# Moving operands read in turn from two halves, two front fillers fewer, and two row blocks begun early, in a hybrid encoder layer

## The chip, the cores and the metric

The kernel runs on one core of one Trainium2 chip. The metric is the device time of one execution in microseconds, and lower is better. Three timed runs of the kernel before gave 859.51, 858.84 and 859.25 us, a median of 859.25.

## The reference

One layer of a bidirectional encoder, on two sequences of 256 tokens (together T = 512 columns) with D = 1024 channels, all in float32. Cut to what matters:

```python
h = rmsnorm(x) ; proj = h @ w_in            # 9952 columns: q|k|v, decays, gates, latents, queries
# branch A: depthwise conv + SiLU on q, k, v; gated delta rule forwards and backwards, 8 heads
o_gdn = rmsnorm(o_fwd + o_bwd) * silu(z_gdn)
# branch B: latent attention, 8 heads, low-rank q and kv, rotary part
o_mla = softmax(q_full @ k_full.T * scale) @ v * silu(z_mla)
# branch C: attention of 4 heads into 256 memory tokens
o_mem = softmax(qx @ km.T * scale) @ vm * silu(z_mem)
merged = (sigmoid(g0) * (o_gdn @ w_br_gdn) + sigmoid(g1) * (o_mla @ w_br_mla)
          + sigmoid(g2) * (o_mem @ w_br_mem))
y = rmsnorm(x + merged @ w_out)
```

## The kernel before

Activations lie feature-major: a tile has 128 channels on the partitions and the 512 tokens of both sequences on the columns. A product `h @ w` is made in row blocks of 128 output channels. Weights and activations are kept as two parts, a rounded high part and the rest (names with `hh`/`hl`, `wh`/`wl`), in the format fp32r, and a product is three passes: high by high, high by low, low by high. So a row block over 1024 input channels is 24 matmuls of 512 columns, `gemm` at line 246. Each has its own stationary 128x128 piece of the weight, and the moving operand is the activation tile.

Each block's weight is loaded by SP (`wr_`, two buffers), rounded by ACT to `wh_` (line 210), and the rest is split off by DVE to `wl_` (line 214). The high part is needed by the block's first 16 matmuls, the low part by the last 8.

There are three stages. The **front** (`front`) makes the memory keys and values, the latents and both attentions. Its PE order is chosen by the scheduling layer from priorities. `fills(n)` takes n row blocks from a list of fillers (`plan`): q/k/v blocks of the delta rule with their convolution (`qkv_tile`), gates (`gate_tile`, names `g`), and so on. These stand between attention steps, so that TensorE has work while ACT and DVE do a softmax. While fillers are made, `prepare` issues a few steps of the first solver preparation (`gdn_prep`): a chain of DVE operations on `tt` and `tm`, 31 rounds long, for four heads each.

The **middle** (`middle`) runs the delta rule. Its PE order is written out by a planner, `weave`: it keeps a planned time, lets each chain (preparation, loads, decays, two solver lanes, output, norm) issue its next step when its planned time has come, and fills the time between with filler matmuls. `gemm` yields the planned cost of each matmul, and a chain step yields its own cost and the delay until its next. `can` says when a filler may start. The names are `kk` for key products, `u`, `xs`, `us`, `x` for solver steps, `o` for a head's output, `so` for its sum of squares, `rob` for the norm row that comes back by way of DRAM (`d_n`), `xg` for the normed head.

The **back** (`back`) multiplies the eight heads `xg` by the first branch's weight (`bg`, eight row blocks), adds up the merge, and runs the output product `y` with the final norm (`output`). `bm` are the second branch's row blocks, `be` the third's. Blocks `bm` and `bg` take their last input channels last, so that late heads hold up only the end of a block.

PSUM has eight banks. In the front, three are for `gm` (gemm outputs), two for `kk`, three for `ms`; from the middle on four are for `gm` and two for each of two `ms` tags.

Of the kernel before, what the change touches and what calls it, by code (L numbers as in the profile page):

```python
# [7 lines left out]
F32 = mybir.dt.float32  # L8
# [5 lines left out]
P = 128  # L14
# [71 lines left out]
def prep(i):  # L86
# [12 lines left out]
    def col(a):  # L99
# [27 lines left out]
        "xT": fm(x), "xn": tm(x), "memT": fm(mem),  # L127
# [29 lines left out]
class Layer:  # L157
# [41 lines left out]
    def weight(self, src, n, name, pool=None):  # L199
# [7 lines left out]
        kw = {} if pool else {"tag": "wh", "bufs": 2}  # L207
        hi = (pool or self.p0).tile([P, 1024], F32R, name="wh_" + name, **kw)
        with self.tc.high_priority(offset=60):
            self.wround = nc.scalar.activation(hi[:, :n], raw[:, :n], AF.Copy).ins  # L210
            kw = {} if pool else {"tag": "wl", "bufs": 2}
            lo = (pool or self.p0).tile([P, 1024], F32R, name="wl_" + name, **kw)
            eng = nc.vector
            d = eng.tensor_tensor(lo[:, :n], raw[:, :n], hi[:, :n].bitcast(F32), op=ALU.subtract)  # L214
            if eng is nc.vector:
                self.wsplit = d.ins
# [17 lines left out]
    def gemm(self, src, nk, xs, name, m=P, ps=None):  # L234
# [10 lines left out]
        for (a, j), k in order:  # L245
            nc.tensor.matmul(ps[:m], a[:, k * m:(k + 1) * m], xs[k][j],  # L246
                             start=n == 0, stop=n == 3 * nk - 1)
            n += 1
            yield 0.234
# [106 lines left out]
    def mem_v(self):  # L356
# [28 lines left out]
        for k, (raw, wr) in enumerate(raws):  # L385
# [10 lines left out]
            for i, (a, b) in enumerate(((0, hi), (1, hi), (0, lo))):  # L396
                for tb in range(4):
                    t = slice(tb * P, (tb + 1) * P)
                    nc.tensor.matmul(vps[tb], ms[k][a][:, t], b[:, :512],  # L399
# [24 lines left out]
    def mem_kt(self, h):  # L424
# [3 lines left out]
            nc.scalar.activation(kt, ps, AF.Copy)  # L428
# [60 lines left out]
    def rotate(self, dst, src, table):  # L489

        n = table.shape[0]
        self.nc.vector.tensor_tensor(dst.rearrange("p (s t) -> p s t", s=2), src.rearrange("p (s t) -> p s t", s=2),
                                     table.unsqueeze(1).to_broadcast([n, 2, 256]), op=ALU.mult)

    def rope_key(self):
# [13 lines left out]
        self.rotate(t[0:64], ps[0:64], cs[0:64])  # L509
        self.rotate(u[0:32], ps[32:64], sn[32:64])  # L510
        self.rotate(u[32:64], ps[0:32], sn[0:32])
# [138 lines left out]
    def mla_rope(self, g):  # L650
# [6 lines left out]
        for j, (p1, p2, op) in enumerate(((pa, pb, ALU.subtract), (pb, pa, ALU.add))):  # L657
            t, u = self.tb("rt"), self.tb("ru")
            self.rotate(t, p1, self.cos)
            self.rotate(u, p2, self.sin)  # L660
# [14 lines left out]
    def mla_v(self, g):  # L675
# [4 lines left out]
        for tb in range(4):  # L680
# [5 lines left out]
            for a, j in ((hi, 0), (hi, 1), (lo, 0)):  # L686
                for k in range(2):
                    nc.tensor.matmul(ps, self.kl[k][j][:, t], a[:, k * 512:(k + 1) * 512],
# [7 lines left out]
    def mla_qk(self, hh, between):  # L696
        A = self.A
        r = []
        for w, nk, xs, n in ((A["w2"], 2, self.kl, "kn"), (A["w3"], 3, self.ql, "qn")):
# [9 lines left out]
            self.split(ps, hi, lo)  # L709
# [39 lines left out]
    def qkv_tile(self, h, part):  # L749
# [4 lines left out]
        if part < 2:  # L754
# [3 lines left out]
            if part == 0:  # L758
                self.k_done.add(h)
            return  # L760
# [854 lines left out]
```

## Time and profile before

| | us |
|---|---|
| median of the timed runs | 859.25 |
| the profiled execution's own time | 859.05 |
| its span in the profile | 857.3 |
| TensorE busy | 845.6 |
| VectorE (DVE) busy | 573.4 |
| ScalarE (ACT) busy | 451.9 |
| GpSimd (POOL) busy | 145.4 |

The span is the time from the first to the last instruction of the core, and the execution's own time has 1.75 us more around it. PE is TensorE's matmuls; PEld are the loads of stationary operands, which run beside them; DVE, ACT, POOL and SP are the vector, scalar, GpSimd and sync engines. Matmuls are pipelined, so a record of 0.4 us can begin 0.23 us after the one before it: what counts is the distance from start to start. In the chain of waits, each row has its start, its length and what ran, followed back from the last instruction. A row of the stage table has the stretch, and for each engine the busy time and the number of instructions in it. In a row of a timeline, the bracket at the end tells how long the engine sat idle before the instruction and what ended that.

### The profile page before, as it was taken

How to read it: one execution, taken by the hardware profiler on the slowest of the kernel's cores; microseconds unless marked ns; L12 is line 12 of the kernel's file. 1: busy time of each engine (PE TensorE's matmuls, PEld its weight loads, DVE VectorE, ACT ScalarE, POOL GpSimd, SP SyncE). 2: the span in 40 equal slices, each digit the busy share in tenths (PEclk: the TensorE clock that was granted, in tenths of full speed). 3: DMA queues.
4: the chain of work that ended last, by engine and by line, in shares of the span. 5: the costliest groups of instructions: out<-in, count | busy, mean ns of one | idle time of the engine just before them, and what ended most of it. 6: DMA issues, size and time to landing. Idle time of an engine off the chain costs nothing.

```text
span 857.3 us, 13230 instructions
## 1 busy us (share of the span) xinstructions
PE 845.6 (99%) x4822; PEld 698.4 (81%) x4822; DVE 573.4 (67%) x1021; ACT 451.9 (53%) x891; POOL 145.4 (17%) x135
## 2 busy tenths in 40 slices
PE   9999999999999999999999999999999999999997
PEld 7878888888888888878788888888888888888886
DVE  7776347687599998457689998684555544346543
ACT  7655455455474465546775748666663632223232
POOL 0200111000100002072101254213110002332121
PEclk9999999999999999999999999999999999999999
DMA  9422222442425525363334365546445447375332
GB/s 326 141 79 87 86 81 68 139 138 75 103 77 164 137 90 146 116 191 129 109 103 122 117 189 174 152 134 180 132 122 160 138 134 250 118 241 160 116 98 99
DMA packets 68273, 116.10 MB, mean 135 GB/s; under 512 B 24048, under 2 KB 31600, under 8 KB 68208
## 3 DMA queue, kind: packets, MB, share of 16 engines
q1 hardware_dynamic: 46560, 104.51, 38.6%
q10 hardware_dynamic: 21648, 10.75, 4.6%
q8 instruction: 38, 0.62, 0.3%
q14 instruction: 27, 0.22, 0.1%
HBM read 95.09 MB, written 16.99 MB: 131 GB/s over the span
## 4 chain that ended last, share of the span: by engine, by line
PE 95%; DVE 2%; ACT 1%; issue 1%; DMA 1%; POOL 0%; POOLq 0%; ACTq 0%; DVEq 0%; SPq 0%
PE gm_qkv L246 16%; PE gm_g L246 16%; PE gm_z L246 8%; PE gm_bm L246 5%; PE gm_bg L246 5%; PE gm_za L246 5%; PE y L1256 5%; PE vm L399 3%; PE gm_be L246 3%; PE gm_qm L246 3%; PE gm_km L246 3%; PE kk L971 3%; PE o L1121 2%; PE gm_qn L246 2%; PE gm_cq L246 2%; PE s_a L308 2%
## 5 line engine op out<-in xcount | busy, mean ns | idle before, releaser
L745 DVE SCALAR_TENSOR_TENSOR kq<-cz,prm,kq 128x510 f32<-128x510 f32 (+1 forms) x64 | 48.1, 752 | 6.0 <-ACT kq L738 5.0
L246 PE MATMUL gm_qkv<-hh,wh_qkv 128*128 128x512 f32 x192 | 51.1, 400 | 0.5 <-ACT wh_qkv L210 0.5
L246 PE MATMUL gm_g<-hl,wh_g 128*128 128x512 f32 x192 | 51.5, 399 | 0.0
L246 PE MATMUL gm_g<-hh,wl_g 128*128 128x512 f32 x192 | 51.3, 398 | 0.0
L246 PE MATMUL gm_g<-hh,wh_g 128*128 128x512 f32 x192 | 51.1, 401 | 0.1
L246 PE MATMUL gm_qkv<-hh,wl_qkv 128*128 128x512 f32 x192 | 50.3, 397 | 0.0
L246 PE MATMUL gm_qkv<-hl,wh_qkv 128*128 128x512 f32 x192 | 49.7, 396 | 0.0
L214 DVE TENSOR_TENSOR wl_qkv<-wr_qkv,wh_qkv 128x1024 fp32r<-128x1024 f32 x24 | 31.1, 1297 | 25.9 <-ACT wh_qkv L210 10.1
L214 DVE TENSOR_TENSOR wl_g<-wr_g,wh_g 128x1024 fp32r<-128x1024 f32 x24 | 30.1, 1254 | 22.0 <-PE gm_g L246 11.7
L246 PEld LDWEIGHTS gm_qkv<-hl,wh_qkv 128*128 128x128 f32 x192 | 35.8, 188 | 8.2
L246 PEld LDWEIGHTS gm_qkv<-hh,wh_qkv 128*128 128x128 f32 x192 | 35.3, 188 | 8.9 <-ACT wh_qkv L210 1.2
L246 PEld LDWEIGHTS gm_qkv<-hh,wl_qkv 128*128 128x128 f32 x192 | 35.5, 188 | 7.8
L246 PEld LDWEIGHTS gm_g<-hl,wh_g 128*128 128x128 f32 x192 | 35.4, 188 | 7.7
L246 PEld LDWEIGHTS gm_g<-hh,wl_g 128*128 128x128 f32 x192 | 35.3, 188 | 7.5
L246 PEld LDWEIGHTS gm_g<-hh,wh_g 128*128 128x128 f32 x192 | 35.1, 188 | 7.8 <-ACT wh_g L210 0.3
L210 ACT ACTIVATE wh_qkv<-wr_qkv 128x1024 fp32r<-128x1024 f32 x24 | 25.4, 1058 | 29.1 <-PE gm_qkv L246 8.6
L1256 PE MATMUL y<-wh_wo,mh 128*128 128x512 f32 (+1 forms) x144 | 39.9, 370 | 0.0
L210 ACT ACTIVATE wh_g<-wr_g 128x1024 fp32r<-128x1024 f32 x24 | 25.4, 1060 | 26.0 <-PE gm_g L246 11.6
L961 POOL TENSOR_TENSOR kl<-kq,kh 128x512 fp32r<-128x512 f32 x16 | 22.8, 1427 | 94.8 <-ACT kh L959 94.8
L1226 POOL TENSOR_TENSOR mg<-mg,lg 128x512 f32<-128x512 f32 x16 | 27.2, 1700 | 59.0 <-DVE lg L1225 59.0
L246 PE MATMUL gm_bm<-xa,wh_bm 128*128 128x512 f32 x128 | 33.5, 398 | 0.0
L246 PE MATMUL gm_bg<-xg,wh_bg 128*128 128x512 f32 x128 | 32.5, 395 | 0.0
(432 smaller groups left out, 2199.5 us busy)
## 6 DMA issues: line engine op xcount, KB each, us to landing
wr_g<-in_w_dram SPq DMA_DIRECT2D x24, 512.0 KB
wr_qkv<-in_w_dram SPq DMA_DIRECT2D x24, 512.0 KB
e<-d_r SPq DMA_DIRECT2D x64, 96.0 KB
wr_z<-in_w_dram SPq DMA_DIRECT2D x12, 512.0 KB
d_g<-gt_g ACTq DMA_DIRECT2D x16, 256.0 KB
wr_za<-in_w_dram SPq DMA_DIRECT2D x8, 512.0 KB
wr_bm<-in_w_dram SPq DMA_DIRECT2D x8, 512.0 KB
lg<-d_g SPq DMA_DIRECT2D x16, 256.0 KB
```

What stands on the lines that cost most here:

```text
L210: self.wround = nc.scalar.activation(hi[:, :n], raw[:, :n], AF.Copy).ins
L214: d = eng.tensor_tensor(lo[:, :n], raw[:, :n], hi[:, :n].bitcast(F32), op=ALU.subtract)
L246: nc.tensor.matmul(ps[:m], a[:, k * m:(k + 1) * m], xs[k][j], start=n == 0, stop=n == 3 * nk - 1)
L308: nc.tensor.matmul(sp[:, qb * 256:(qb + 1) * 256], a, b, start=j == 0, stop=j == n - 1)
L399: nc.tensor.matmul(vps[tb], ms[k][a][:, t], b[:, :512], start=k == 0 and i == 0, stop=k == 7 and i == 2)
L745: nc.vector.scalar_tensor_tensor(ys, zs, self.cw[:, f, m:m + 1], ys, ALU.mult, ALU.add)
L961: nc.gpsimd.tensor_tensor(lo, src, hi.bitcast(F32), op=ALU.subtract)
L971: nc.tensor.matmul(ps, a[:, k], b, start=i == 0, stop=i == 2)
L1121: nc.tensor.matmul(out, ub[:, d, s, cp], rhs, start=n == 0, stop=n == 3)
L1226: nc.gpsimd.tensor_tensor(self.merged[d], self.merged[d], gt, op=ALU.add)
L1256: nc.tensor.matmul(ps, xs[2 * j + q][a][:, t], b[:, q * 512 + c0:q * 512 + c1], start=j == 0 and n == 0, stop=j == 3 and n == 5)
```

## The change

Three things are changed.

First, matmuls with a moving operand of 512 columns read it in the order 0, 256, 1, 257, ... (`turns`): a column from the first half, then one from the second. The output is still written to consecutive places of PSUM (`pairs`). Where the host can store the operand with its even columns first and its odd columns second (`_halves`: the tokens x, and the weights that move), the output comes out in its natural order. Elsewhere (memory keys, the latent products, key products, branch products, the decay product) it comes out with the halves interleaved, and the operation that reads it from PSUM takes every second column (`unpaired`). The planner books 0.217 us a matmul for 0.234, and 0.65 for 0.70 for three key products. Matmuls of 256 or 128 columns are as they were, but for the last two half-width output products, which are read in turn too.

Second, in the second half of the latent attention only heads 4 and 6 take a filler.

Third, the first branch's row blocks 0 and 1 start as fillers at the end of the middle, as soon as head 6 is normed (`bg_begin`, 21 of 24 matmuls), and take head 7 at the end (`bg_end`). Block 0's weight takes two buffers tagged `y32`. With it come three gates of the planner: the second preparation waits until a planned time, `load_xe` waits for that preparation, and `branch_mem` for the split of its operand.

```diff
+def _halves(a):
+    return np.concatenate([a[..., 0::2], a[..., 1::2]], -1)
...
-        w.reshape(k // 256, 2, P, c // 512, 512).transpose(3, 0, 2, 1, 4)).reshape(
+        _halves(w.reshape(k // 256, 2, P, c // 512, 512)).transpose(3, 0, 2, 1, 4)).reshape(
...
+def turns(x):
+    return x.rearrange("p (c s) -> p s c", c=2)
+def pairs(x):
+    return x.rearrange("p (s c) -> p s c", c=2)
+def halves(x):
+    return x.rearrange("p (c s) -> p c s", c=2)
+def unpaired(x):
+    return x.rearrange("p (s c) -> p c s", c=2)
...
-        "xT": fm(x), "xn": tm(x), "memT": fm(mem),
+        "xT": _halves(fm(x)), "xn": tm(x), "memT": fm(mem),
...
-            nc.tensor.matmul(ps[:m], a[:, k * m:(k + 1) * m], xs[k][j],
+            nc.tensor.matmul(pairs(ps[:m]), a[:, k * m:(k + 1) * m], turns(xs[k][j]),
                              start=n == 0, stop=n == 3 * nk - 1)
             n += 1
-            yield 0.234
+            yield 0.217
...
-            nc.scalar.activation(kt, ps, AF.Copy)
+            nc.scalar.activation(halves(kt), unpaired(ps), AF.Copy)
...
-            self.split(ps, hi, lo)
+            self.split(unpaired(ps), halves(hi), halves(lo))
...
                 self.k_done.add(h)
+                self.k_at = self.now + 8.0
...
-                    nc.tensor.matmul(ps, a[:, k], b, start=i == 0, stop=i == 2)
-                pc.append(ps.rearrange("p (a t) -> p a t", a=2))
-                yield 0.70, 6.0 * cch
+                    nc.tensor.matmul(pairs(ps), a[:, k], turns(b), start=i == 0, stop=i == 2)
+                pc.append(unpaired(ps))
+                yield 0.65, 6.0 * cch
...
-        nc.vector.scalar_tensor_tensor(gt, gt, 1.0, ps, ALU.add, ALU.mult)
+        nc.vector.scalar_tensor_tensor(halves(gt), halves(gt), 1.0, unpaired(ps), ALU.add, ALU.mult)
...
+    def bg_begin(self, d):
+        nc = self.nc
+        gt = self.gate_in(0, d)
+        hi, lo = self.weight(self.A["w8"][C_BG + d], 1024, f"bg{d}", None if d else self.pg, "y32")
+        ps = self.ps_gm(f"gm_bg{d}")
+        parts = [(p, k) for p in ((hi, 0), (hi, 1), (lo, 0)) for k in range(8)]
+        parts.sort(key=lambda o: o[1] >= 7)
+        self.begun[d] = gt, ps, parts[21:]
+        for n, ((a, j), k) in enumerate(parts[:21]):
+            nc.tensor.matmul(pairs(ps), a[:, k * P:(k + 1) * P], turns(self.xg[k][j]), start=n == 0, stop=False)
+            yield 0.217
+
+    def bg_end(self, d):
+        gt, ps, parts = self.begun[d]
+        for n, ((a, j), k) in enumerate(parts):
+            self.nc.tensor.matmul(pairs(ps), a[:, k * P:(k + 1) * P], turns(self.xg[k][j]), start=False, stop=n == 2)
+        self.gated(d, gt, ps)
...
-                    nc.tensor.matmul(ps, xs[2 * j + q][a][:, t], b[:, q * 512 + c0:q * 512 + c1],
+                    nc.tensor.matmul(pairs(ps), xs[2 * j + q][a][:, t],
+                                     turns(b[:, q * 512:(q + 1) * 512])[:, c0 // 2:c1 // 2],
...
         self.fill += [(self.branch, 1, d, self.xa, A["w8"][C_BM:], "bm") for d in range(8)]
+        self.fill += [(self.bg_begin, d) for d in range(2)]
...
-                fills(1)
+                if not g or h in (0, 2):
+                    fills(1)
...
+            for d in range(2):
+                self.bg_end(d)
...
-        while any(h not in self.k_done for h in range(4, 8)):
+        while any(h not in self.k_done for h in range(4, 8)) or self.now < self.k_at:
...
+        if f == self.load_xe:
+            return self.pr[1]
         if f == self.split_x:
-            return self.now > self.xe_at
+            return len(self.xe) == 4 and self.now > self.xe_at
+        if f == self.bg_begin:
+            return 6 in self.xg
+        if f == self.branch_mem:
+            return self.xe_split
...
-        for d in range(8):
+        for d in range(2, 8):
             _finish(self.branch(0, d, xg, self.A["w8"][C_BG:], "bg"))
```

The same pair of `turns` and `pairs` stands in the memory values, the latent values and the decay product, and the same `unpaired` in the third branch's merge, the rotary products and the decay sum.

More of the change, by code (lines that the diff above doesn't have):

```diff
@@ L196, in c, with weight @@
         return self.cst[:, lo:hi]
-    def weight(self, src, n, name, pool=None):
+    def weight(self, src, n, name, pool=None, tag=None):
         nc = self.nc
@@ L206, in weight, with place @@
             self.after = d.ins
-        kw = {} if pool else {"tag": "wh", "bufs": 2}
-        hi = (pool or self.p0).tile([P, 1024], F32R, name="wh_" + name, **kw)
+        def place(t, own):
+            kw = {"tag": own, "bufs": 2} if own else {}
+            return (pool or self.p0).tile([P, 1024], F32R, name=t + name, **kw)
+        hi = place("wh_", tag if pool else "wh")
         with self.tc.high_priority(offset=60):
             self.wround = nc.scalar.activation(hi[:, :n], raw[:, :n], AF.Copy).ins
[L211 to L216, printed above, removed]
+            lo = place("wl_", tag if pool else "wl")
+            self.wsplit = nc.vector.tensor_tensor(lo[:, :n], raw[:, :n], hi[:, :n].bitcast(F32),
+                                                  op=ALU.subtract).ins
         return hi, lo
@@ L398, in mem_v @@
                     t = slice(tb * P, (tb + 1) * P)
-                    nc.tensor.matmul(vps[tb], ms[k][a][:, t], b[:, :512],
+                    nc.tensor.matmul(pairs(vps[tb]), ms[k][a][:, t], turns(b[:, :512]),
                                      start=k == 0 and i == 0, stop=k == 7 and i == 2)
@@ L491, in rotate @@
         n = table.shape[0]
[L492 to L493 removed]
+        self.nc.vector.tensor_tensor(halves(dst), src, table.unsqueeze(1).to_broadcast([n, 2, 256]), op=ALU.mult)
     def rope_key(self):
@@ L687, in mla_v @@
                 for k in range(2):
-                    nc.tensor.matmul(ps, self.kl[k][j][:, t], a[:, k * 512:(k + 1) * 512],
+                    nc.tensor.matmul(pairs(ps), self.kl[k][j][:, t], turns(a[:, k * 512:(k + 1) * 512]),
                                      start=n == 0, stop=n == 5)
@@ L808, in gdn_prep @@
             for i in range(2):
-                nc.tensor.matmul(dp, self.bd, rhs[i], start=i == 0, stop=i == 1)
-            nc.vector.tensor_tensor(ed, ed, dp, op=ALU.add)
+                nc.tensor.matmul(pairs(dp), self.bd, turns(rhs[i]), start=i == 0, stop=i == 1)
+            nc.vector.tensor_tensor(halves(ed), halves(ed), unpaired(dp), op=ALU.add)
             nc.scalar.activation(ed, ed, AF.Exp)
@@ L1224, in gated @@
         nc = self.nc
-        nc.vector.scalar_tensor_tensor(gt, gt, 1.0, ps, ALU.add, ALU.mult)
+        nc.vector.scalar_tensor_tensor(halves(gt), halves(gt), 1.0, unpaired(ps), ALU.add, ALU.mult)
         nc.gpsimd.tensor_tensor(self.merged[d], self.merged[d], gt, op=ALU.add)
@@ L1356, in plan @@
         vt = [(self.v_tokens, h) for h in range(8)]
+        self.xe_split, self.begun, self.k_at = False, {}, 0.0
         self.xe, self.xa, self.xa_at, self.xa_raw, A = [], [None] * 8, {}, {}, self.A
@@ L1562, in split_x @@
     def split_x(self, xs):
+        self.xe_split = True
         with self.tc.issue_after(self.wround):
```

10 lines of the change are left out of this document (5 added, 5 removed).

## The prediction

> **What bounds the kernel now.** I read the page's busy times first, then its chain, then the waits of TensorE, and last a table by stages.
>
> ```profile
> span 857.3 us, 13230 instructions
> ...
> PE 845.6 (99%) x4822; PEld 698.4 (81%) x4822; DVE 573.4 (67%) x1021; ACT 451.9 (53%) x891; POOL 145.4 (17%) x135
> ...
> DVE  7776347687599998457689998684555544346543
> ...
> PE 95%; DVE 2%; ACT 1%; issue 1%; DMA 1%; POOL 0%; POOLq 0%; ACTq 0%; DVEq 0%; SPq 0%
> ```
>
> TensorE has work for all but 11.7 us of the span and carries 95% of the chain. So the time is the sum of the matmuls' spacings, and what makes one matmul shorter makes the kernel shorter, until another engine is late. The DVE row says where that will be: two stretches of nines. In the stage table (engines in the order PE, PEld, DVE, ACT, POOL; then clock, DMA share, GB/s):
>
> ```profile
> 0.00:20.00 20.00, 17.86 (x68) 13.88 (x69) 15.26 (x26) 13.95 (x24) 0.33 (x5) 1.00 0.92 321
> 240.00:340.00 100.00, 98.80 (x505) 82.70 (x504) 92.75 (x184) 57.30 (x115) 5.75 (x4) 1.00 0.43 122
> 340.00:370.00 30.00, 29.01 (x160) 24.36 (x160) 15.27 (x28) 18.23 (x39) 2.21 (x3) 1.00 0.42 132
> 420.00:540.00 120.00, 120.00 (x887) 99.22 (x886) 110.45 (x220) 75.98 (x168) 35.66 (x31) 1.00 0.46 141
> ```
>
> DVE is at 93% and 92% there. In the first of them it has already decided once: the chain leaves TensorE for DVE work that began before this row and ends, through ACT, at a rounded weight:
>
> ```profile
> 246.71 1.16 DVE xx L865
> ...
> 256.83 1.07 ACT wh_g L210
> ```
>
> **The change, part by part.** *Reading in turn.* The chain gives the spacing of 512-column matmuls where they run undisturbed, and rows of other shapes:
>
> ```profile
> 300.80 2.14 PE s_a L308 x18
> ...
> 507.18 2.62 PE o L1121 x16
> ...
> 761.19 44.80 PE gm_bg L246 x192
> 805.99 39.12 PE y L1256 x168
> ```
>
> 44.80/192 = 233.3 ns and 39.12/168 = 232.9 ns. The s_a matmuls have 256 columns and take 2.14/18 = 119 ns, about half of 233: the time goes with the columns, 0.456 ns each, and is no fixed cost per instruction. The o matmuls read plain fp32:
>
> ```profile
> L1121 PE MATMUL o<-e,ub 128*128 128x256 f32 x64 | 19.3, 383 | 0.0
> ...
> L1121 PE MATMUL o<-e,ub 128*128 128x128 f32 x64 | 12.3, 274 | 0.0
> ```
>
> Each head has 8 records of 256 and 8 of 128 columns, 3072 columns in 2.62 us, 0.853 ns each. If plain fp32 passes each column twice (the trace doesn't say so), a pass takes 0.426 ns, and 512 of them 218 ns. So the array can go faster than 0.456 ns when columns are asked for more slowly; something that feeds it at full rate holds back some 15 ns in 512. The read of the moving operand is the candidate that the change touches: two streams 1 KiB apart, a column of each in turn. The PSUM side stays contiguous. No row shows such a read, so its price is open from both sides: 218 ns is the low end from the rows, and the high end is the dearest step in the trace, DVE's write with a step of 128 bytes, against the same work contiguous:
>
> ```profile
> L856 DVE TENSOR_TENSOR dd<-nd,kd x2: 1087/1099/1111, 240.1 to 427.3; 128x512 f32<-128x512 f32 x2
> ...
> L810 DVE TENSOR_TENSOR ed<-ed,dp 128x512 f32<-128x512 f32 x4 | 2.7, 683 | 0.4 <-PE dp L809 0.4
> ```
>
> 1099/683 = 1.61, so 233 would become 375 ns. I take 217 ns: within a nanosecond of the low end, and the cost that the changed planner itself books. The Trainium skill, "TensorE: Matmul & The Clock Gate", section "Wait — 56ns, not 53.3ns?", measures 215.7 ns for back-to-back matmuls of 512 columns; this trace shows 233, and by the page's figure the sum would gain 4 us more.
>
> How many: line 246 has one row,
>
> ```profile
> 0.00:858.00 858.00, 647.48 (x2604) 479.21 (x2604) 1.00 0.43 135
> ```
>
> and the code's loops add 96 (vm, L399), 48 (v, L688), 96 (kk, L971), 8 (dp, L809), 168 of y and 48 half-width ones of y that count as 24: 3044 in all. 3044 × (233.2 − 217) = **49.3 us less**. The ten zp matmuls, scores, o and the small ones stay.
>
> *What of it is lost.* (a) In the first 20 us DMA runs at 0.92 share and the 96 vm matmuls take their loads as they land: 96 × 16.2 ns = 1.6 us, of which I count 1.0 as lost. (b) Between 240 and 340 TensorE would need 5.5 us less (317 of line 246 and 24 of line 688), 94.5, and DVE still has 92.75 to do in strict order with its own waits. The lead of the split weight is small there:
>
> ```profile
> 285.73 1.22 DVE L214 TENSOR_TENSOR wl_g<-wr_g,wh_g 128x1024 fp32r<-128x1024 f32 x1
> ...
> 289.44 2.03 PE L246 MATMUL gm_g<-hh,wl_g 128*128 128x512 f32 x8
> ...
> 484.38 1.43 DVE L214 TENSOR_TENSOR wl_g<-wr_g,wh_g 128x1024 fp32r<-128x1024 f32 x1
> ...
> 492.24 0.63 PE L246 MATMUL gm_g<-hh,wl_g 128*128 128x512 f32 x2
> ```
>
> 289.44 − 286.95 = 2.5 us. Of the 5.5 us I count 3.0 as lost. (c) Between 420 and 540 TensorE would need about 7 us less (375 of line 246, some 55 kk), 113, against 110.45 of DVE; the lead at 492 is 6.4 us, so I count 2.0 as lost.
>
> *Two front fillers fewer.* The fillers at heads 5 and 7 fall away, so the last two, gates g04 and g05, become the first work of the middle; 48 matmuls, two 512 KB loads and two 256 KB stores move with them, none goes. They no longer cover the front's end. TensorE there, before (oa7 is the last attention product, gm_za7 a gate's block, gm_qkv12 the middle's first):
>
> ```order
> L246 MATMUL gm_za7_3615<-hh5_370,wl_za7_3613 128x512
> L246 MATMUL gm_za7_3615<-hh6_377,wl_za7_3613 128x512
> L334 MATMUL pt_a70_3666<-cst_309,p_a70_3658 128x128
> L246 MATMUL gm_za7_3615<-hh7_384,wl_za7_3613 128x512
> L334 MATMUL pt_a70_3666<-cst_309,p_a70_3658 128x128 x3
> L334 MATMUL pt_a71_3704<-cst_309,p_a71_3696 128x128 x4
> L343 MATMUL oa7_3642<-ph_a70_3671,vh10_2836 128x256
> ```
>
> and with the change:
>
> ```order
> L334 MATMUL s_a71_3607<-ks21_667,qs21_2688 128x256
> L369 MATMUL oa6_3455<-ph_a61_3522,vh12_2903 128x256
> ...
> L369 MATMUL oa6_3455<-ph_a61_3522,vl13_2915 128x256
> L360 MATMUL pt_a70_3592<-cst_309,p_a70_3584 128x128 x4
> L369 MATMUL oa7_3568<-ph_a70_3597,vh10_2836 128x256
> L360 MATMUL pt_a71_3630<-cst_309,p_a71_3622 128x128
> ...
> L272 MATMUL gm_g04_3698<-hh0_337,wh_g04_3694 128x512
> ```
>
> All of gm_za7 now stands ahead of the last scores, so only matmuls that need those softmaxes are left to run beside them. From before, the last score and what follows it:
>
> ```profile
> 361.78 0.28 PE L308 MATMUL s_a<-ks,qs 128*128 128x256 f32 x1
> ...
> 362.10 0.69 DVE L311 TENSOR_REDUCE mx_a<-s_a 128x2 f32<-128x512 f32 x1 [1.48 <-PE s_a L308]
> ...
> 366.07 0.49 ACT L328 ACTIVATE p_a<-p_a,rs_a 128x256 f32<-128x256 f32 x1
> ...
> 366.62 0.55 PE L334 MATMUL pt_a<-cst,p_a 128*128 128x128 f32 x3 [0.55 <-ACT p_a L328]
> ...
> 367.86 0.38 PE L343 MATMUL oa<-pl_a,vh 128*128 128x256 f32 x1 [0.37 <-DVE pl_a L224]
> ...
> 369.28 2.03 PE L246 MATMUL gm_qkv<-hh,wh_qkv 128*128 128x512 f32 x8
> ```
>
> The last score's start to the next free matmul is 7.5 us, of which before had about 1.8 us of gaps. Afterwards the same chain has 18 products at 0.12 and 8 transposes at 0.11 beside it, 3.0 us: about 4.5 to 5 us of gaps, **3.0 us more**.
>
> *Two row blocks begun early.* bg0 and bg1 run 21 of their 24 matmuls on heads 0 to 6 and get head 7 later, so that head 7 is covered by 46 matmuls instead of 21. Before, bg0's 21 matmuls stand ahead of its three on xg7. With the change:
>
> ```order
> L1269 MATMUL gm_bg1_7694<-xg6_7503,wl_bg1_7692 128x512
> L272 MATMUL gm_bg2_7749<-xg0_5263,wh_bg2_7745 128x512
> ...
> L272 MATMUL gm_bg2_7749<-xg3_6471,wh_bg2_7745 128x512
> L1276 MATMUL gm_bg0_7664<-xg7_7719,wh_bg0_7660 128x512
> L272 MATMUL gm_bg2_7749<-xg4_6816,wh_bg2_7745 128x512
> ```
>
> On SP's queue, however, head 7's norm (d_n) is moved behind the load of bg2, which before came three rows after it:
>
> ```order
> L229 DMA wr_bg1_7688<-in_w8_dram 128x1024
> L1239 DMA lg_17_7608<-d_g_68 128x512
> L229 DMA wr_bg2_7743<-in_w8_dram 128x1024
> L1239 DMA lg_00_7656<-d_g_68 128x512
> L316 DMA d_n_66<-rt_3664 4x32 x4
> L229 DMA wr_bg3_7778<-in_w8_dram 128x1024
> ```
>
> That load needs wr_bg0's buffer, which DVE's split of bg0 frees; the split writes a y32 buffer that xa5 holds until matmul 22 of bm7 (blocks 5 to 7 come last there). Behind d_n wait the loads of bg3 and the output's rows, which have time; on ACT the rounding of bg2 now stands ahead of the load of head 7's norm. Count from bm7's start: 22 × 0.217 + 0.8 (so7) + 1.2 (split) + 0.7 (two issues) = 7.5 us for d_n. The rest is in before:
>
> ```profile
> 752.06 1.27 SPq L290 DMA_DIRECT2D d_n<-rt  x4
> 755.22 0.33 ACTq L295 DMA_DIRECT2D rob<-d_n  x1
> 758.58 0.69 DVE L1153 TENSOR_TENSOR og<-og,rob 128x512 f32<-128x512 f32 x1 [1.13 <-DMA rob<-d_n]
> 759.30 0.63 ACT L222 ACTIVATE xg<-og 128x512 fp32r<-128x512 f32 x1 [3.32 <-DVE og L1153]
> ```
>
> 759.93 − 752.06 = 7.9, so xg7 is there at 15.4. TensorE wants it after 24 + 46 matmuls and so7, at 16.0. I count 0.5 us lost, 0 to 2.
>
> *Reads of PSUM with a step of 8 bytes* (kk, kn, qn, rope, kmt, be, bm, bg). No row shows one. Low end 0, since DVE's columns ask for less than half of TensorE's rate; high end L856's 0.42 us per 512 columns. I take 0, which is nearer to how the L810 row reads PSUM.
>
> *The planner's costs and gates.* A matmul is booked at 0.217 us for 0.234, and a chain step's delay stays in us, so more filler matmuls stand between two steps and about the same time. The second solver preparation waits 8 us of planned time, load_xe for that preparation, branch_mem for the split. These are waits of the planner, not of an engine: they only reorder, other fillers stand there, and I price them at 0; without fillers left they would cost up to the 8 us once.
>
> Sum, against this execution's 859.05 us: −49.3 + 1.0 + 3.0 + 2.0 + 3.0 + 0.5 = −39.8, **819 us**. The execution is 0.2 us under the median of 859.25, which changes nothing.
>
> **Rivals.** *DVE becomes the bound* (stepped PSUM reads at the high price). Per head kk has 3072 such columns, 2.5 us; three heads fall in 420 to 540, 7.5 us on 110.45, over TensorE's 113 by 5; between 240 and 340 some ten reads of 512 add 4 us. With the ends and the rest, 12 us more: 831. For it: 93% now. Against: leads of 6 us and more outside.
>
> *No gain in the read*: what holds 0.456 ns is the PSUM write, untouched. Then the 3.0 at the front's end and perhaps 0.5 at the join remain: 863, **slower by 0.4%**. The losses pay off as soon as a matmul gains over 9.5 us / 3044 = 3 ns.
>
> *The stepped read costs*: at 375 ns a matmul, 3044 × 142 ns = 432 us more, 1290. This speaks against the change by a rule: the Trainium skill, "SBUF — State Buffer", section "Door 1", says that SBUF gives full rate to accesses that stay in a 16-byte line and makes each crossing pay, and here every access leaves the line of the one before. The DVE row L856 agrees in kind; no run here shows TensorE's read. Against: each of the two streams still walks its line in order.
>
> *Half of the gain*: 225 ns, 25 us of the 49.3 with less lost: 838.
>
> **How the numbers follow.** Forecast 0.68 (811 to 828: a spacing of 215 to 219, the losses from 5 to 15 us), DVE 0.15, half 0.05, no gain 0.07 (0.02 of it within 0.2%, about what a measurement of this kernel can tell from no change), stepped read 0.05. Faster 0.88, same 0.02, slower 0.10. The range takes the forecast, the DVE case and half: 806 to 842.
>
> **What would show it.** The whole matmuls of gm_bg and y at 217 ns each, against 233. A gap of TensorE near the front's end ahead of oa7 by several us; waits of PE on DVE or ACT between 225 and 325, and fewer between 390 and 505; a PE wait on xg under 2 us; L982 at 476 and 341 ns as before if stepped PSUM reads are free. The forecast is wrong if the spacing stays over 225, or if DVE's groups grow.

## The result, and the profile after

The kernel after takes **832.0 us**, median of four runs (830.73 to 834.47), against 859.38 us for the kernel before in four runs (858.84 to 860.04). The ratio is 0.9685, with a 95% interval of 0.9661 to 0.9708: faster by 3.2%. The forecast was 819.0 in a range of 806 to 842. The direction and the read's gain held; the time is 13 us above the forecast, since more of the gain was lost than the sum had.

First the page of the kernel after, whose profiled execution took 832.2 us: the span, the busy times, VectorE's forty slices, the clock's, and the shares of the chain.

```profile
span 830.4 us, 13228 instructions
...
PE 804.7 (97%) x4822; PEld 704.4 (85%) x4822; DVE 570.2 (69%) x1021; ACT 448.1 (54%) x891; POOL 142.2 (17%) x135
...
DVE  7786457778699988446889997848574464546643
...
PEclk9999999999999999799999999999999999999998
...
PE 79%; DVE 8%; DMA 5%; ACT 3%; issue 2%; SPq 1%; ACTq 0%; POOL 0%; POOLq 0%; DVEq 0%
```

TensorE now stands still for 25.7 us of the span instead of 11.7, and it has 79% of the chain instead of 95%. VectorE, DMA and ScalarE, which had 2, 1 and 1%, have 8, 5 and 3%. The other engines' busy times hardly moved. The clock's row shows a 7, one slice (332 to 353 us) that was not at full clock; the 8 is the kernel's end, behind the last products. Next the chain's rows with the spacing (start, length, what):

```profile
317.94 1.08 PE s_a L334 x9
...
752.55 29.79 PE gm_bg L272 x138
782.34 36.27 PE y L1302 x168
```

29.79/138 and 36.27/168 are both 215.9 ns, where before had 233. The scores (1.08/9 = 120 ns) were left as they were and stay. At the 17 ns gained per matmul, 3044 of them give 52 us. So some 25 us of it are lost again, and the stage table says where (PE, PEld, DVE, ACT, POOL; clock, DMA share, GB/s):

```profile
240.00:340.00 100.00, 96.35 (x512) 85.53 (x510) 88.09 (x179) 56.26 (x113) 6.19 (x5) 0.98 0.47 137
340.00:370.00 30.00, 27.23 (x115) 22.75 (x116) 9.60 (x15) 14.96 (x33) 17.61 (x25) 0.83 0.56 171
420.00:540.00 120.00, 114.34 (x767) 99.08 (x768) 108.50 (x213) 73.26 (x160) 37.46 (x30) 1.00 0.47 138
```

In the second row, the front's end, the granted clock is 0.83 on average. In the third TensorE is idle for 5.7 of 120 us, where before had none.

For a finer account I worked out, from the start times of all matmuls of each trace, how much later each one starts than its predecessor's undisturbed spacing allows (216 ns for 512 columns in turn, 233 contiguous, 119 for 256 columns, 111 for 128), and added up what exceeds 60 ns. A matmul at half clock counts with what it takes too long. The account is that of one profiled execution of each kernel, whose own time stands beside the median. Five stages, us:

| kernel | median | profiled | 0–200 | 200–300 | 300–400 (front's end) | 400–640 (middle) | from 640 | sum |
|---|---|---|---|---|---|---|---|---|
| before | 859.4 | 859.1 | 6.7 | 2.6 | 2.9 | 8.1 | 2.6 | 22.9 |
| after | 832.0 | 832.2 | 9.2 | 5.8 | 10.9 | 18.7 | 2.2 | 46.8 |
| contiguous, all else as after (e4) | 869.3 | 870.0 | 6.8 | 3.5 | 10.4 | 9.5 | 3.1 | 33.3 |
| read in turn alone (e3) | 817.5 | 817.6 | 8.9 | 5.4 | 3.5 | 13.2 | 1.6 | 32.5 |
| + new planner costs (e5) | 830.0 | 830.2 | 8.9 | 5.2 | 3.3 | 18.9 | 8.6 | 44.9 |
| + planner costs raised (e11) | 825.0 | 825.0 | 8.9 | 5.4 | 3.5 | 20.9 | 1.1 | 39.8 |
| + planner waits (e6) | 825.7 | 827.5 | 8.9 | 4.7 | 3.5 | 23.1 | 2.0 | 42.2 |
| + two front fillers fewer (e7) | 832.6 | 832.4 | 9.5 | 5.5 | 11.7 | 18.3 | 1.9 | 46.8 |
| + two blocks begun early (e8) | 820.5 | 820.1 | 9.5 | 5.4 | 3.6 | 14.8 | 1.5 | 34.9 |
| after, fillers put back (e1) | 829.0 | 827.4 | 8.6 | 5.2 | 3.3 | 18.3 | 6.7 | 42.1 |
| after, no early blocks (e2) | 835.4 | 834.4 | 8.9 | 5.4 | 11.4 | 19.9 | 3.4 | 48.9 |

The rows below the first two are the experiments. After lost 23.9 us more than before: 8.0 at the front's end, 10.6 in the middle, 5.7 ahead of 300, and nothing from 640 on. The profiled time less the sum is 836 to 837 us in the two kernels that read contiguously and 785.1 to 785.6 us in all nine that read in turn, so the read is worth about 51 us in every one of them, and the rest of each difference lies in these stages.

**The front's end.** The chain there, after (start, length, what):

```profile
334.65 3.44 DMA d_xa<-za
...
338.18 0.61 ACT za L1188
...
344.09 0.58 PE oa L369
...
348.30 1.44 PE oa L369 x5
349.74 0.43 PE gm_g L272
```

In ScalarE's order za at 338.18 stands ahead of the last two softmaxes, and it waits for a store (d_xa, 3.44 us) to release its tile. Nothing free is left for TensorE beside them, and the five products at 348.30, 120 ns each elsewhere, take 1.44 us: the clock is down. The windows of 3.41 us around it, in the columns of the stage table:

```profile
338.12:341.53 3.41, 1.35 (x7) 0.83 (x6) 2.06 (x6) 2.78 (x8) 0.54 (x1) 1.00 0.38 135
341.53:344.95 3.42, 2.16 (x7) 1.29 (x7) 1.58 (x5) 2.89 (x9) 0.00 (x0) 0.50 0.22 77
344.95:348.36 3.41, 2.58 (x11) 1.88 (x10) 0.69 (x1) 1.44 (x3) 2.00 (x2) 0.50 0.21 47
348.36:351.77 3.41, 3.41 (x11) 2.96 (x12) 0.69 (x1) 0.20 (x1) 3.26 (x4) 0.50 0.89 249
```

After the window in which TensorE was busy for 1.35 of 3.41 us, three windows run at 0.50. The 26 matmuls that start in them need 3.6 us at full clock, so up to 3.6 of the 7.4 us lost against the kernel with the read alone are the clock.

**The middle.** TensorE's longest wait there is on VectorE. From the timeline of after:

```profile
496.44 1.23 DVE L905 STREAM_TRANSPOSE o<-ts 128x1024 f32<-128x1024 f32 x1
...
498.61 1.23 DVE L907 STREAM_TRANSPOSE o<-tt 128x1024 f32<-128x1024 f32 x1
...
499.77 0.95 DVE L1008 SCALAR_TENSOR_TENSOR e<-e,cc,kk 128x128 f32<-128x128 f32 x3
...
500.21 0.45 PE L997 MATMUL kk<-kh 128*128 128x512 f32 x1 [2.77 <-DVE e L1008]
```

kk at 500.21 needs a PSUM bank that VectorE still reads; between the reads VectorE's order has two transposes of 1.23 us each. VectorE is not full over the whole stretch (108.50 of 120 above); it is late at single places that its order makes.

The reads of PSUM with a step of 8 bytes cost nothing, as forecast: line 1008 (982 before) on 256 columns,

```profile
L1008 DVE SCALAR_TENSOR_TENSOR na<-e,cc,kk 128x256 f32<-128x256 f32 x32 | 15.2, 474 | 3.6 <-PE kk L997 3.5
```

474 ns against 475 before:

```profile
L982 DVE SCALAR_TENSOR_TENSOR na<-e,cc,kk 128x256 f32<-128x256 f32 x32 | 15.2, 475 | 8.2 <-PE kk L971 8.1
```

### The profile page after: what moved, and what is told of

The parts are those of the page before. It is cut to its first block, busy times and chain, and to the rows that moved or that the text cites. A ratio compares the mean times of both kernels' runs of the same rounds, so it can differ in the third digit from the quotient of the medians.

```text
span 830.4 us, 13228 instructions
## 1 busy us (share of the span) xinstructions
PE 804.7 (97%) x4822; PEld 704.4 (85%) x4822; DVE 570.2 (69%) x1021; ACT 448.1 (54%) x891; POOL 142.2 (17%) x135
## 4 chain that ended last, share of the span: by engine, by line
PE 79%; DVE 8%; DMA 5%; ACT 3%; issue 2%; SPq 1%; ACTq 0%; POOL 0%; POOLq 0%; DVEq 0%
PE gm_g L272 13%; PE gm_qkv L272 12%; PE gm_bm L272 5%; PE gm_z L272 5%; PE y L1302 4%; PE gm_bg L272 4%; PE gm_za L272 4%; PE vm L425 3%; PE gm_qm L272 3%; PE gm_be L272 3%; PE gm_km L272 2%; PE o L1147 2%; PE gm_cq L272 2%; PE s_a L334 2%; PE kk L997 2%
## 5 line engine op out<-in xcount | busy, mean ns | idle before, releaser
L241 DVE TENSOR_TENSOR wl_g<-wr_g,wh_g 128x1024 fp32r<-128x1024 f32 x24 | 30.2, 1259 | 30.5 <-ACT wh_g L239 13.2
L272 PE MATMUL gm_qkv<-hh,wh_qkv 128*128 128x512 f32 x192 | 47.7, 384 | 3.3 <-ACT wh_qkv L239 1.8
L272 PE MATMUL gm_g<-hh,wh_g 128*128 128x512 f32 x192 | 48.9, 392 | 0.7 <-ACT wh_g L239 0.7
L272 PE MATMUL gm_qkv<-hh,wl_qkv 128*128 128x512 f32 x192 | 47.8, 383 | 0.0
L272 PE MATMUL gm_g<-hl,wh_g 128*128 128x512 f32 x192 | 47.8, 383 | 0.0
L272 PE MATMUL gm_g<-hh,wl_g 128*128 128x512 f32 x192 | 47.2, 382 | 0.0
L272 PE MATMUL gm_qkv<-hl,wh_qkv 128*128 128x512 f32 x192 | 46.7, 381 | 0.0
L1302 PE MATMUL y<-wh_wo,mh 128*128 128x512 f32 (+1 forms) x144 | 37.7, 356 | 0.0
L272 PE MATMUL gm_bm<-xa,wh_bm 128*128 128x512 f32 x128 | 31.3, 382 | 0.0
L1302 PEld LDWEIGHTS y<-wh_wo,mh 128*128 128x128 f32 x144 | 26.1, 190 | 3.1
```

What stands on the lines that cost most here:

```text
L241: self.wsplit = nc.vector.tensor_tensor(lo[:, :n], raw[:, :n], hi[:, :n].bitcast(F32), op=ALU.subtract).ins
L272: nc.tensor.matmul(pairs(ps[:m]), a[:, k * m:(k + 1) * m], turns(xs[k][j]), start=n == 0, stop=n == 3 * nk - 1)
L1302: nc.tensor.matmul(pairs(ps), xs[2 * j + q][a][:, t], turns(b[:, q * 512:(q + 1) * 512])[:, c0 // 2:c1 // 2], start=j == 0 and n == 0, sto ...
```

## The experiments

Twelve kernels were run. Theory A, ahead of the first: the read in turn gives the whole gain, the missing cover costs the front's end, and the middle's loss is VectorE's. Its rivals: part of the gain comes from the order; the front's end is late for another reason; the middle's loss comes from what the planner was told.

**Each part of the change undone, or the read done alone**

```diff
 # e1_fill: after, with
-                if not g or h in (0, 2):
-                    fills(1)
+                fills(1)
 # e2_nobg: after, with
-        self.fill += [(self.bg_begin, d) for d in range(2)]
...
-            for d in range(2):
-                self.bg_end(d)
...
-        for d in range(2, 8):
+        for d in range(8):
 # e3_turns_only: after, with both of these and
-            yield 0.217
+            yield 0.234
...
-                yield 0.65, 6.0 * cch
+                yield 0.70, 6.0 * cch
...
-        while any(h not in self.k_done for h in range(4, 8)) or self.now < self.k_at:
+        while any(h not in self.k_done for h in range(4, 8)):
...
-        if f == self.load_xe:
-            return self.pr[1]
...
-            return len(self.xe) == 4 and self.now > self.xe_at
+            return self.now > self.xe_at
...
-        if f == self.branch_mem:
-            return self.xe_split
 # e4_contig: after, with turns, pairs and _halves giving back their argument, and unpaired a split into halves
```

> The kernel before with the read in turn alone: fillers, row blocks, planner costs and planner waits as before. Theory A: spacing of the 512-column matmuls 216 ns as in the kernel after, no half clock at the front's end, gaps of the middle about as in the kernel after (10 to 15 us, since they come from VectorE and from fixed latencies and not from the order): 820 to 828 us. Rival (the other parts are what brings the gain of the middle): over 832 us. Rival (the other parts only cost): under 818 us.

Measured: **817.45 us** (816.14 to 817.57), ratio 0.9506 (0.949 to 0.9522). The read alone beats the kernel after by 14.5 us. The time is the second rival's (the other parts only cost), and theory A's 820 is missed, though its spacing and its front's end hold. Its chain has

```profile
726.31 41.44 PE gm_bg L272 x192
```

215.8 ns a matmul, as in after. Its front's end has 3.5 us of gaps and no half clock, the middle 13.2.

> The kernel after with every matmul reading and writing contiguous columns, all else (order of the work, planner costs and waits) as in the kernel after. Theory A (the read is the whole gain): spacing back at 232 to 233 ns, the front's end still loses some 7 us with a half clock, the middle loses little since VectorE has 17 ns more per matmul: 864 to 870 us. Rival (the order brings part of the gain): under 857 us.

Measured: 869.31 us (867.01 to 869.97), ratio 1.011 (1.0095 to 1.0125), inside theory A's band. The y row of its chain is 816.89 to 856.01 us, 39.12/168 = 232.9 ns as before. So without the read the change is 1.1% slower than before, 7.5 us of it at the front's end (10.4 against 2.9 us). The middle, in the same planned order as after, loses only 1.4: that order becomes dear only with the shorter matmuls. (The prediction's rival "no gain in the read" said 863.)

> The kernel after with the two front fillers put back (a filler at every head). Theory A (the read gives 52 us; the front's end loses 7.3 us because no free matmul is left beside the last softmaxes, part of it because the granted clock falls to half behind the gaps): the gaps of 320 to 360 us fall from 10.0 to under 4 us, the half clock there goes, the middle has two fillers less, and the time is 825 to 828 us. Rival (the front's end is late because VectorE lags, fillers or not): the gaps stay at 8 us or more and the time is 831 to 834 us. Rival (the two gates are missed in the middle more than at the front): over 834 us.

Measured: 828.98 us (826.34 to 832.36), ratio 0.9647 (0.9618 to 0.9677). At its own place theory A is right: in the same stretch of e1 and of after stand

```profile
320.00:360.00 40.00, 38.89 (x221) 34.65 (x220) 21.43 (x34) 23.35 (x46) 11.75 (x11) 1.00 0.57 168
```

```profile
320.00:360.00 40.00, 35.85 (x182) 30.75 (x181) 20.83 (x35) 19.25 (x41) 16.62 (x20) 0.87 0.58 168
```

The gap and the low clock go with the fillers. But the time falls by 3.0 us and not by theory A's 4 to 7: from 640 on, e1 has 4.5 us more of gaps (a solver step, us, waits 2.6 us for w, and 3.4 us at half clock follow). The two gates moved into the middle seem to have been cover there.

> The kernel after without the two row blocks begun early; the gates of the planner, the two fillers fewer and the read in turn stay. Theory A (the early blocks keep TensorE busy while head 7 is normed): a gap of 2 to 4 us ahead of the first matmul on head 7, 833.5 to 836 us. Rival (head 7 is hidden anyway by 21 matmuls of the first block): 831 to 833 us. If the fillers' shift moves the middle as well, its gaps change by more than 2 us and the time says nothing of the join alone.

Measured: 835.44 us (834.16 to 836.63), ratio 0.972 (0.9706 to 0.9735). The time is theory A's, the place is not. TensorE's only wait beyond 700 us is

```profile
PE gm_bg L272 <- ACT wh_bg L239: 0.6, 1, 0.6
```

on a weight, not on head 7. Head 7 was hidden without the early blocks, as the rival said. The 2 us by which the account is longer than after's lie in the middle (1.2) and from 640 on (1.2), and are not explained.

**One more part on top of the read alone**

```diff
 # each is e3_turns_only (817.45 us) with one part of the change put back
 # e5_turns_217: the costs 0.217 and 0.65
 # e6_gates: the planner's waits (k_at, load_xe, split_x, branch_mem)
 # e7_fewer: fills(1) only if not g or h in (0, 2)
 # e8_early: bg_begin and bg_end for blocks 0 and 1
 # e11_cost25: the costs 0.25 and 0.75
```

> The read in turn with the planner's new costs (0.217 and 0.65 for 0.234 and 0.70) and nothing else of the change. The read alone with the old costs took 817.5 us. Theory A (the costs only reorder, price 0): 816 to 819 us, gaps of 440 to 580 us within 2 us of the 9.4 us that the read alone has there. Rival (the middle of the kernel after loses because the planner, told of shorter matmuls, puts the solver's steps elsewhere): 821 us or more with gaps of 440 to 580 us over 12 us.

Measured: **829.96 us** (828.04 to 830.82), ratio 0.9651 (0.9634 to 0.9669). The rival holds: the two numbers, which make no instruction, cost 12.5 us. Its waits of TensorE from 640 us on:

```profile
PE gm_bg L272 <- ACT xg L248: 3.4, 1, 3.4
PE us L1123 <- DVE w L1118: 1.5, 1, 1.5
```

Head 7 is now late. Why shows in the solver's last products and the first matmul of bg, first for the read alone, then with the new costs (least, middle and longest ns, first and last start):

```profile
L1147 PE MATMUL o<-e,ub x128: 272/327/483, 452.9 to 702.3; 128*128 128x256 f32 x64, 128*128 128x128 f32 x64
...
L272 PE MATMUL gm_bg<-xg,wh_bg x128: 379/379/379, 726.1 to 767.2; 128*128 128x512 f32 x128
```

```profile
L1147 PE MATMUL o<-e,ub x128: 272/327/382, 461.3 to 718.8; 128*128 128x256 f32 x64, 128*128 128x128 f32 x64
...
L272 PE MATMUL gm_bg<-xg,wh_bg x128: 379/379/483, 734.1 to 779.8; 128*128 128x512 f32 x128
```

The last o starts 16.5 us later, and 15.3 us of other work stand behind it instead of 23.8. A delay of the chain is booked in us, so a cheaper booked matmul puts more matmuls beside each delay, and they are missing at the end. The traces' counts agree: between the last o and the first bg stand 106 matmuls of 512 columns in the read alone, 66 with the new costs, and 199 with the costs raised (next run).

> The read in turn alone, with the planner's costs raised to 0.25 and 0.75 (0.234 and 0.70 took 817.5 us, 0.217 and 0.65 took 830.0 us). A delay of the solver's chain is booked in us, so a dearer booked matmul puts fewer real matmuls beside it and more of them are left for the end. Theory A (the booked cost decides how the fillers are shared out: too low and they run out before the last head, too high and the steps come before their inputs are there): no gap beyond 660 us, gaps of 440 to 580 us over the 9.4 us of 0.234, 817 to 823 us. Rival (a dearer booking is better throughout): gaps of 440 to 580 us under 8 us, under 816 us. Rival (any order but the old one loses, whichever way the cost is moved): over 825 us, with gaps at places that neither of the others has.

Measured: 825.0 us (824.07 to 825.5), ratio 0.9594 (0.9578 to 0.961). Raising the costs goes the other way, as theory A has it: the last o at 689.6 us, 43.9 us ahead of bg, and only 1.1 us of gaps from 640 on. In return the solver's steps come before their inputs:

```profile
PE kk L997 <- DVE e L1008: 4.4, 2, 4.0
PE p L1048 <- DVE na L1008: 1.5, 1, 1.5
```

The middle loses 20.9 us. The size is 2 us over theory A's band, at the edge of the third rival, and two points about 0.234 can't tell an optimum of the cost from an order that happens to fit.

> The read in turn with the planner's waits (the second solver preparation 8 us of planned time later, the loads of xe after it, the memory branch after the split) and nothing else of the change. Theory A (waits of the planner only reorder, price 0): 816 to 819 us. Rival (they move VectorE's work of the middle together): 821 us or more, the gaps of 440 to 580 us over 12 us. Of this run and the one with the new costs, the slower one names the part that costs the middle; if both stay under 819.5 us, the middle's loss is the fillers' shift or needs several parts together.

Measured: 825.71 us (825.36 to 827.45), ratio 0.9611 (0.9596 to 0.9626): 8.3 us lost. The rival holds, and the place is kk again, and two stretches of 3.4 us at half clock follow gaps in the middle, at 493 and 565 us:

```profile
PE kk L997 <- DVE e L1008: 5.6, 3, 2.3
```

> The read in turn with two front fillers fewer and nothing else of the change. Theory A (the front's end loses 6 to 9 us: gaps of 320 to 360 us go from 2.6 to 8 us or more, and the clock halves behind them for 10 us; the gates run later in the middle at no price): 823 to 827 us. Rival (two gates more in the middle cover its waits and give the loss back): 817 to 820 us.

Measured: 832.57 us (831.24 to 833.84), ratio 0.9687 (0.967 to 0.9705). The front's end loses 8.2 us as theory A said, but its 823 to 827 is missed: the two gates are not free in the middle either, which loses 5.1 more, with two stretches of 3.4 us at half clock, at 415 and 494 us: 15 us in all.

> The read in turn with the two row blocks begun on heads 0 to 6 and nothing else of the change. Theory A (with the old order TensorE has no gap ahead of head 7, since the read alone shows under 0.4 us of gaps beyond 680 us): 816 to 819 us, no difference from the read alone. Rival (the early blocks cover more than that): under 815.5 us. Rival (the norm of head 7 behind the load of the third block comes late): a gap ahead of the first matmul on head 7 and over 819 us.

Measured: 820.49 us (818.76 to 822.38), ratio 0.9547 (0.9528 to 0.9565). All three are missed: TensorE waits for nothing beyond 700 us, so neither cover nor delay at head 7 decides; 1.6 us are lost in the middle and 0.6 ahead of 200 us. A half clock of 3.4 us falls at 243 us, but its stage loses no more than in the read alone (5.4 us in both).

The costs of the parts do not add up: alone on top of the read they lose 12.5, 8.3, 15.1 and 3.0 us, together 14.5. The new costs let the fillers run out early, and the moved gates and the early blocks seem to bring some back: from 640 on 8.6 us are lost with the new costs alone, 6.7 in e1, 3.4 in e2 and 2.2 in after.

**The read by itself**

```diff
 # m1_reads: one line for each, 48 matmuls into one bank, no other engine at work
+nc.tensor.matmul(ps, ws(i), x[:, 512:], ...)                      # L58 contiguous
+nc.tensor.matmul(pairs(ps), ws(i), two(h), ...)                   # L55 two halves, 1 KiB apart
+nc.tensor.matmul(pairs(ps), ws(i), two(x)[:, :256], ...)          # L61 two halves, 2 KiB apart
+nc.tensor.matmul(ps.rearrange("p (s c) -> p s c", c=4), ws(i), four(h), ...)   # L64 four quarters
+nc.tensor.matmul(ps.rearrange("p (c s) -> p c s", c=2), ws(i), step2(h), ...)  # L67 step of 8 bytes
```

> A kernel by itself, without the layer: it computes none of the reference. On an idle chip it runs, line by line, 48 matmuls of 512 columns rounded to fp32r with the moving operand read contiguously, in turn from two halves (1 KiB apart), in turn from two halves of a tile twice as long (2 KiB apart), in turn from four quarters, with a step of 8 bytes, in turn from two streams 128 bytes apart and from two streams 16 bytes apart; the same with 256 columns; 16 matmuls in plain fp32, contiguous, in turn and with a step of 8 bytes on both sides; and reads of PSUM by VectorE and ScalarE, contiguous and with a step of 8 bytes. Theory A (the moving operand's read holds the contiguous stream back, and two places far apart lift it): contiguous 232 to 234 ns, two halves 215 to 217 ns at either distance, quarters the same, step of 8 bytes 217 ns or more, PSUM reads alike. Rival (it is the kernel's other engines on SBUF that hold the contiguous read back): contiguous 216 to 218 ns here. Rival (a line that is left costs): step of 8 bytes and 16 bytes apart over 240 ns.

Measured, in the chain of waits (182.06 us in one run; L70 is two streams 128 bytes apart, L74 16 bytes apart, L78 and L81 are 256 columns contiguous and in turn, L84, L87 and L90 plain fp32 with a step of 8 bytes, contiguous and in turn, two records a matmul):

```profile
20.20 10.36 PE ps L55 x48
30.56 10.91 PE ps L58 x48
41.47 10.36 PE ps L61 x48
51.83 13.59 PE ps L64 x48
65.42 21.65 PE ps L67 x48
87.07 10.36 PE ps L70 x48
97.44 10.36 PE ps L74 x48
107.80 5.75 PE ps L78 x48
113.55 5.36 PE ps L81 x48
118.91 14.40 PE ps L84 x32
133.31 13.73 PE ps L87 x32
147.04 17.29 PE ps L90 x32
```

In turn 215.8 ns at any distance, 16 bytes included; contiguous 227.3. So the operand's read holds the contiguous stream back, by 11.5 ns here, where no other engine works, and by some 17 in the layer; reading in turn takes both away. The second theory (the other engines hold it back) wanted 216 to 218 contiguous and is refuted. It does not explain the other 6 ns either: in the kernel before, 43 spacings between 512-column matmuls have no instruction of VectorE, ScalarE or GpSimd and no DMA packet beside them, and they average 233 ns like the rest. What makes the 6 ns stays open. Quarters take 283 ns against theory A, a step of 8 bytes 451. The third theory is right for the step and wrong for 16 bytes. 256 columns gain 8 ns (119.8 to 111.7). Plain fp32 loses in turn (540 for 429 ns a record). VectorE's and ScalarE's reads of PSUM take 686 and 597 ns with or without a step.

**Two attempts at the waits**

```diff
 # e9_za: e3_turns_only, with
-        z = self.ta(f"za{h}")
+        z = (self.s2 if h % 2 else self.ta)(f"za{h}")
 # e10_pool: after, with, from the middle on,
+                nc.gpsimd.tensor_tensor(lo[:, :n], raw[:, :n], hi[:, :n].bitcast(F32), op=ALU.subtract)
```

> The read in turn alone (817.5 us), with the gate tiles za of every other head of the second branch in the five buffers of s2 instead of the two of ta. Theory A (at 245 us ScalarE stands in order behind a gate tile whose buffer the store to d_xa still holds, and the rounded weight behind it is late): the gap of 2.0 us ahead of gm_g at 245 us goes, and the time falls by 1.5 to 3 us, 814.5 to 816 us. Rival (VectorE is what is late there): the gap stays, 816.5 to 818.5 us. Rival (the buffers of s2 are missed by the solver's tiles): over 819 us.

Measured: 818.2 us (815.72 to 818.59), ratio 0.9523 (0.9507 to 0.9539). TensorE's wait ahead of gm_g at 245 us went from 1.8 to 0.2 us, so the buffer was its cause; the wait of oa for za just ahead of it grew from 1.5 to 2.1 us. The profiled execution has 30.8 us of gaps against 32.5 and took 815.72 us against 817.57, as theory A has it. But it is the shortest of the four; the other three took 817.92 to 818.59 us at granted clocks of 0.995 to 0.997, against 0.998. So the time as a whole did not fall, and why the others are longer is not shown.

> The kernel after with the splits of the weights in the middle and the back (wl, 1.23 us each on VectorE) given to GpSimd. Theory A (the middle's gaps are VectorE's: it has 19.7 of 20 us to do in its busiest stretches): VectorE's busy time of 440 to 580 us falls by a quarter, the gaps there go from 15 us to under 8 us, and the time is 823 to 827 us. Rival (the gaps come from fixed latencies of the solver's chain, not from VectorE's load): gaps of 440 to 580 us stay over 12 us, 830 us or more. Rival (GpSimd slows VectorE down while it runs, as the 2.49 us of one xg beside a copy suggests, or takes longer than the lead of the weights): VectorE's instructions grow and the time is over 835 us.

Measured: 856.01 us (852.23 to 860.3, ten runs), ratio 0.9967 (0.9949 to 0.9986). The third rival holds, on both of its counts. A split takes GpSimd about twice as long as VectorE's 1.22 us, and VectorE's own instructions grow, first e10 and then after:

```profile
L242 POOL TENSOR_TENSOR wl_g<-wr_g,wh_g 128x1024 fp32r<-128x1024 f32 x20 | 47.7, 2385 | 48.5 <-ACT wh_g L239 30.4 <-PE gm_g L275 13.7 <-issue 2.8
...
L773 DVE SCALAR_TENSOR_TENSOR kq<-cz,prm,kq 128x510 f32<-128x510 f32 (+1 forms) x64 | 60.3, 943 | 33.2 <-ACT kq L766 32.4
```

```profile
L770 DVE SCALAR_TENSOR_TENSOR kq<-cz,prm,kq 128x510 f32<-128x510 f32 (+1 forms) x64 | 47.6, 744 | 8.5 <-ACT kq L763 7.8
```

The mean hides two kinds: the 46 of these 64 instructions that ran beside no GpSimd instruction took 744 ns, as in after, and the 18 that overlapped one took 1451 ns on average, up to 2949. VectorE's busy time of 440 to 580 us fell from 113.9 to 100.1 us, an eighth and not a quarter, and the gaps of the middle grew to 45.5 us. Whether less work for VectorE alone would close the middle's gaps stays open.

The version to keep is the read alone, 817.45 us, 4.9% under the kernel before.

## Why the prediction was right, and where its sum was off

The measured 832.0 us lies in the range of 806 to 842, but outside the 811 to 828 that the prediction gave to its own account; the range reaches it because it also took in the DVE case and half of the gain. So the direction and the read's gain were understood, and that the time fell into the range is in part owed to its width: the losses were 23.9 us, against 5 to 15.

- **Reading in turn: right, and a little too low.** Forecast 217 ns and 49.3 us, from the rate of plain fp32 in line 1121. Measured 216 ns, some 52 us by count, of which about 51 appear in the balance of times. The read alone and its undoing (817 and 869 us) show that it is the whole gain. That the operand's read holds the contiguous stream back is now shown by a kernel of its own. The way to 218 ns was in part luck: plain fp32 leaves two records a matmul (32 for 16 in m1_reads, 16 for a head's eight products), so the 3072 columns of a head had already counted each column twice, at 0.84 to 0.85 ns a record's column. That a record passes its columns twice once more, which the 0.426 ns needs, no run shows, and read in turn plain fp32 gets slower (540 for 429 ns a record). The Trainium skill, "TensorE: Matmul & The Clock Gate", section "Wait — 56ns, not 53.3ns?", gives 215.7 ns: reading in turn reaches that here, and the contiguous read does not, with no other engine at work either (227.3).
- **The stepped read costs (1290 us): wrong.** The rule behind it, the Trainium skill's "SBUF — State Buffer", section "Door 1", would make every change of line pay. Streams 16 bytes apart, which change line with every column, run at 215.8 ns, so it does not hold for two streams; four at 283 and a step of 8 bytes at 451 do pay. The measurement decides.
- **Reads of PSUM with a step: right,** 474 ns against 475.
- **(a), the first 20 us:** forecast 1.0, measured about 0.6. From 160 to 180 us another 1.9 are lost, which the sum did not have.
- **(b), the first stretch of nines:** forecast 3.0, measured 3.2 (200 to 300 us; 3.9 in the forecast's own 240 to 340). The place was right, the cause in part: oa waits for VectorE's za, but gm_g for a weight that ScalarE rounds late behind a gate tile's buffer (e9_za shows it for the read alone), and 3.4 us at half clock follow, which the sum did not have.
- **(c), the second stretch, mis-sized, and with the wrong cause:** forecast 2.0, measured 10.6 over the whole middle (7.4 in the forecast's own 420 to 540 us). Half of it (5.1) comes with the read alone; the other 5.5 only with the other parts. The forecast took VectorE's free time over the whole stretch and the lead of one weight; the longest waits stand at single places, kk above all, where VectorE's order puts the last read of a PSUM bank behind other work. That this makes the whole 10.6 us is not shown.
- **The planner's costs and waits, priced at 0: the step that failed.** The prediction said that they "only reorder". Alone on top of the read they cost 12.5 and 8.3 us, more than any loss in the sum, with no instruction added. The argument that delays in us mean "about the same time" overlooked that the fillers are a fixed stock: what stands beside one step is missing behind the last (66 matmuls left for 106). For the waits, the cost is measured and its place is kk, but how they lead to it was not traced.
- **The front's end: right in mechanism, mis-sized.** Forecast 3.0, measured 8.0. The working counted 7.5 us from the last score to the next free matmul; it is 11.6 here (337.95 to 349.53). ScalarE's wait for a store ahead of the softmaxes, and three windows at half clock behind the gap, were not in it.
- **The join with head 7:** forecast 0.5 lost, measured none. The early blocks were not needed for it either.

With the read's 51 and the losses of 23.9, the time comes out at 832; the forecast had 49.3 and 9.5. Of the rivals, "DVE becomes the bound" (831) meets the number by another way: its cause, dear stepped reads, is refuted.

## What to carry to other kernels

Where TensorE is the bound and its moving operand is fp32r, measure the spacing of matmuls and try a read in turn from two halves: it cost nothing on the reader's side here. Where an order is planned with booked durations, change the bookings in a run of their own, since a truer number may make a worse order. And keep some free matmuls beside each last softmax: a gap there can be paid twice, once as idle time and once as half clock.

## What the runs showed of the hardware that was not expected

The half clock in mid-kernel comes in stretches of 3.41 us or two, three or four times that (13.65 us once, in e10_pool), and always begins on a raster of 3.413 us counted from the first full clock of the run: in after, its two stretches begin 69 and 98 steps of that raster behind it. In after a gap of 1.70 us at 240.0 lies inside one window of the raster, with some smaller ones (2.2 us idle of 3.41 by the spacing of starts):

```profile
239.14:242.55 3.41, 1.81 (x13) 1.27 (x12) 3.41 (x10) 2.45 (x7) 0.00 (x0) 1.00 0.45 137
242.55:245.96 3.41, 3.41 (x14) 3.03 (x13) 3.01 (x10) 1.45 (x4) 0.00 (x0) 0.50 0.28 97
```

The read alone has the same gap, 1.69 us at 239.8, but its raster has a border at 240.66, and no half clock follows:

```profile
237.25:240.66 3.41, 2.77 (x21) 2.19 (x19) 3.41 (x9) 1.70 (x4) 0.00 (x0) 1.00 0.02 6
240.66:244.07 3.41, 2.45 (x17) 2.34 (x18) 3.41 (x10) 2.76 (x8) 0.00 (x0) 1.00 0.60 225
```

Over the traces of this case, a drop from full clock in mid-kernel always followed a window with about 2.0 us or more of idle time so counted (2.01 us at 239.03 in e1_fill), and no window with more than 2.12 us (at 745.20 in e5_turns_217) went without one; between the two both occur. (The busy times of the rows overlap in the pipeline and sort less cleanly.) So the same kernel can lose some us or not, by where its start falls on the raster. The four runs of e8_early fit this: 818.76, 820.09, 820.89 and 822.38 us, at mean granted clocks of 0.998, 0.997, 0.996 and 0.994; not every kernel's runs sort so (e6_gates). The Trainium skill, "TensorE: Matmul & The Clock Gate", section "What's actually happening", has this window, free-running, as 3413 ns, which the stretches agree with; its table lowers the clock after an idle window, and here one that was idle for about 60% was enough.

VectorE's instructions grow where they overlap one of GpSimd's splits: the same line took 744 ns in e10_pool where no GpSimd instruction ran beside it, and 1451 ns on average where one did.
